# The last recurrent head of a hybrid decoder layer in steps of two block sizes

## The chip, the core and the metric

The kernel runs on one core of a Trainium2 chip. A core has five engines, each with its own in-order instruction queue: TensorE (PE; its weight loads are listed as PEld), VectorE (DVE), ScalarE (ACT), GpSimd (POOL) and SyncE (SP, which here issues nearly all transfers). They wait for one another through semaphores. Matmul results land in PSUM, in eight banks of 128 x 512 f32; everything else that is worked on lies in SBUF. The metric is the device time of one execution in microseconds.

## The reference

One decoder layer over 1024 tokens of width 1024, all in float32. After a normalisation, one projection feeds two mixers: dilated sliding-window attention of 8 heads, and a gated linear recurrence (HGRN2) of 4 heads of width 128. Their outputs are joined, projected and added to x; a squared-ReLU feed-forward layer follows. The recurrence, per head:

```python
def step(state, xs):                     # one chunk of C tokens
    qc, kc, vc, gc = xs                  # gc: log of the forget gate
    b = jnp.cumsum(gc, axis=2)
    o_inter = einsum('bhtk,bhkv->bhtv', qc * exp(b), state)
    decay = exp(where(causal, b_t - b_s, -inf))
    a = einsum('bhtk,bhsk,bhtsk->bhts', qc, kc, decay)
    o = o_inter + einsum('bhts,bhsv->bhtv', a, vc)
    new_state = exp(b_last) * state + einsum('bhsk,bhsv->bhkv', kc * exp(b_last - b), vc)
```

The kernel takes chunks of 128 tokens. What the change touches is how the 128 x 128 matrix `a` of a chunk, with its decay between every pair of tokens, is built.

## The kernel before

**Splits.** Large products run in three passes of a 32-bit format: both operands are split into a high and a low part (`split_into`, L85: ACT copies the high part, DVE subtracts, L87), and `three_pass` (L89 to L92) multiplies high x high, high x low, low x high. Weights stream in through `w_load` (L107) and `w_split`; `w_get` (L148) sees to it that a given weight block is split, each split being one long ACT and one long DVE instruction.

**Fillers.** The order of all engines is the order of the program text. Projections are Python generators in a `queue`; each yields after one unit (three matmuls of 128 x 512, booked at 650 ns, or 330 ns in `hgrn_ig`). `fill(ns)` (L195) lets the generators run until the booked costs reach `ns`; a debt or excess is carried on. A generator that yields `None` is blocked, and `fill` stops there. `drain` runs the queue empty.

**Recurrent heads.** For head h, `hgrn_core(h)` runs while the queue holds the projections of head h + 1 (`hgrn_ig`, evacuated by ACT at L421 and L422, and `hgrn_qf`, evacuated by DVE). For the last head, h = 3, the queue holds `attn_proj(0)` and `attn_proj(1)`, the projections of the first two pairs of attention heads, and all fills are scaled by 1.15. In `hgrn_core`: diagonal of `a` (L510, L511), then the climb over block sizes 1, 2, 4, ... 64, then the transposes of k (L615), the states (L623 to L629), the outputs `po` (L643, L645) with their squares (`ysq`, L647) and sums (`hss`, L648), and for the last head `open_attention`, which starts the scores of attention head 0 (`look`, L901, L902, read by DVE at L906; exponent on ACT, L959).

**The climb, two forms.** Between two neighbouring blocks of size c the entries of `a` are k times q, each scaled by running products of the gates.
- *By levels* (L584 to L609, last head): for each of seven sizes, 8 matmuls with 64 columns into one "s" bank (L593), then on DVE: scale half of k (L597), half of q (L599), multiply the totals (L603), and copy the wanted entries under a mask into `at` (L604). Then a fill: 3700, 2900, 2900, then 2200 four times.
- *Two sizes per step* (L519 to L583, heads 0 to 2): `quarter_sets` (L472) lays three operand sets side by side, per half four chunks wide, with two ACT copies and two DVE products (L483 to L490). A step is 8 matmuls with 192 columns into four banks (L529; tags "s", "t", "pv" in turn), the DVE products on q, totals, the next step's sets and k (L542 to L556), and twelve masked copies (L561), then two calls of `table_part` and two fills of 3500. Three steps cover sizes 1 to 32; size 64 is 8 matmuls of 64 x 64 (L572), an ACT copy (L574), three DVE products and a fill of 3400.

A matmul in f32 is issued as two passes, so 8 matmuls are 16 instructions in the profile.

**Attention projections.** `attn_proj(pr)` (L785) projects, for a pair, the queries in two halves (`aq`), the first half of the values (av), the keys in two halves (ak), then the second half of the values: 48 units a pair. Each half is 8 units in one bank with tag "mm" (two banks), which DVE reads out: queries at L806, values at L823, keys at L740. A buffer with tag "half" (two) receives it; for queries and keys ACT writes the high part into a second `half` buffer (`hiq`, `hik`, L733), POOL the low part (L734), and SP moves them into slabs (queries L811, L812; keys L750). Values are turned on PE into an "mm" bank (`pvt`, L773), four units into the next job, and read by ACT and DVE (L776, L777). `attn_proj(1)` blocks after its first half of the values until step 3 of attention.

**Slabs.** SBUF rows of 4 KB come from tags with a fixed number of buffers. Tag S has nine: in the last head it holds q, k, the totals and `at`, two queries per pair and four key slabs.

**After the last head** come 64 attention steps (L1349 on), each with a listed number of units (`UNITS`), one `fill(0.0, True)` per unit. Step 47 drains the queue and puts in the first part of the output projection; steps 44 to 48 also split weights for it on ACT and DVE (L140, L141).

Of the kernel before, what the change touches and what calls it, by code (L numbers as in the profile page):

```python
# [8 lines left out]
F32 = mybir.dt.float32  # L9
F32R = mybir.dt.float32r  # L10
U8 = mybir.dt.uint8
AF = mybir.ActivationFunctionType
ALU = mybir.AluOpType
# [4 lines left out]
P = 128  # L18
T = 1024
D = 1024  # L20
NK = D // P
NT = T // P
# [4 lines left out]
HH = 4  # L27
LEVELS = (1, 2, 4, 8, 16, 32, 64)
# [9 lines left out]
def hymba_layer(ctx, tc, x, w_in, w_out, w_ff1, w_ff2, g_pre, lb_logits, g_mix, g_post,  # L38
# [13 lines left out]
    def slab(tag, name, dtype=F32, shape=(P, T)):  # L52
        return sp.tile(list(shape), dtype, tag=tag, name=name,
                       bufs={"S": 9, "T": 9, "P": 3, "BT": 2, "V8": 2, "R": 1}[tag])

    def bank(tag, name):
        return ps.tile([P, 512], F32, tag=tag, name=name,
                       bufs={"mm": 2, "s": 2, "t": 2, "pv": 2}[tag])
# [136 lines left out]
    def fill(ns, least=False):  # L195
        debt[0] += ns
        if least:
            debt[0] = max(debt[0], 1.0)
        while debt[0] > 0 and queue:
            try:  # L200
                cost = next(queue[0])
            except StopIteration:
                queue.pop(0)
                continue
            if cost is None:
                break
            debt[0] -= cost
        debt[0] = min(debt[0], 0.0)
# [292 lines left out]
    def hgrn_core(h, scale, after=None):  # L501
        hd = heads[h]
        inat, gate, prod, qt, kt, tot = (hd[n] for n in ("inat", "gate", "prod", "qt", "kt", "tot"))
        ready = quarter_sets(hd, h, 0, tot) if h < HH - 1 else None
        fill((5900 if 0 < h < HH - 1 else 5200) * scale)
        at = slab("S", f"at{h}", F32, (P, NT, P))
        for hf in range(2):
# [7 lines left out]
            nc.sync.dma_start(out=gcols, in_=g_mix.rearrange("(k p) -> p k", p=P))  # L515
        if h == HH - 1:
            load_bias(0)
        if h < HH - 1:
            fill(1200 * scale)  # L519
            totals = slab("P", f"tot{h}")  # L520
            for step in range(3):
                c = 4 ** step
                nb = 32 // c
                sets, cv = ready
                banks4 = []
                for u in range(4):
                    pl = bank(("s", "t", "pv")[(2 * step + u // 2) % 3], f"pl{h}_{step}{u}").rearrange("p (n q) -> p n q", n=2)
                    for n in range(2 * u, 2 * u + 2):
                        TE.matmul(pl[:, n % 2, :192], kt[:, n * P:(n + 1) * P], sets[u // 2][:, n % 4],  # L529
                                  start=True, stop=True)  # L530
                    banks4.append(pl)
                w = T // (4 * c)
                at_ = (0, 768, 960)[step]
                tots = totals[:, at_:at_ + 3 * w].rearrange("p (i w) -> p i w", i=3)
                u23, u123, nx = (tots[:, i] for i in range(3))
                cw = cv.rearrange("p n b f -> p (n b) f")
                q4 = qt.rearrange("p (m f c) -> p m f c", f=4, c=c)
                k4 = kt.rearrange("p (m f c) -> p m f c", f=4, c=c)

                def spread(ap, k=c):  # L540
                    return ap.unsqueeze(2).to_broadcast([P, w, k])
                V.tensor_tensor(out=q4[:, :, 1], in0=q4[:, :, 1], in1=spread(cw[:, :, 0]), op=ALU.mult)  # L542
                for hf in range(2):
                    n4 = slice(hf * 4, hf * 4 + 4)
                    V.tensor_tensor(out=qt[:, hf * 512:hf * 512 + 512].rearrange("p (n b f c) -> p n b (f c)", n=4, f=4, c=c)
                                    [:, :, :, 2 * c:],
                                    in0=sets[hf][:, :, 128:].rearrange("p n (b w) -> p n b w", b=nb),
                                    in1=cv[:, n4, :, 0:1].to_broadcast([P, 4, nb, 2 * c]), op=ALU.mult)
                V.tensor_tensor(out=u23, in0=cw[:, :, 2], in1=cw[:, :, 3], op=ALU.mult)
                V.tensor_tensor(out=u123, in0=cw[:, :, 1], in1=u23, op=ALU.mult)  # L550
                V.tensor_tensor(out=nx, in0=cw[:, :, 0], in1=u123, op=ALU.mult)
                if step < 2:
                    ready = quarter_sets(hd, h, step + 1, nx)
                V.tensor_tensor(out=k4[:, :, 2], in0=k4[:, :, 2], in1=spread(cw[:, :, 3]), op=ALU.mult)
                V.tensor_tensor(out=k4[:, :, 1], in0=k4[:, :, 1], in1=spread(u23), op=ALU.mult)
                V.tensor_tensor(out=k4[:, :, 0], in0=k4[:, :, 0], in1=spread(u123), op=ALU.mult)  # L556
                for u, pl in enumerate(banks4):
                    for part_, mask, c2 in ((0, masks[:, 2 * step], c), (2, masks[:, 2 * step + 1], 2 * c),
                                            (1, near[:, step], 2 * c)):
                        av = at[:, 2 * u:2 * u + 2].rearrange("p n (b two c) -> p n b two c", two=2, c=c2)  # L560
                        V.copy_predicated(  # L561
                            av[:, :, :, 1, :],
                            mask.rearrange("p (b c) -> p b c", c=c2).unsqueeze(1).to_broadcast([P, 2, 64 // c2, c2]),
                            pl[:, :, part_ * 64:part_ * 64 + 64].rearrange("p n (b c) -> p n b c", c=c2))
                cur = nx
                table_part()
                fill(3500 * scale)
                table_part()
                fill(3500 * scale)
            pl = bank("s", f"pl{h}_6")  # L570
            for n in range(NT):
                TE.matmul(pl[:64, n * 64:(n + 1) * 64], kt[:, n * P:n * P + 64], qt[:, n * P + 64:(n + 1) * P],  # L572
                          start=True, stop=True)
            S.activation(at[:64, :, 64:], pl[:64].rearrange("p (n c) -> p n c", n=NT), AF.Copy)  # L574
            kv, qv = (x.rearrange("p (n two c) -> p n two c", two=2, c=64) for x in (kt, qt))
            cv = cur.rearrange("p (n two) -> p n two", two=2)
            V.tensor_tensor(out=qv[:, :, 1], in0=qv[:, :, 1], in1=cv[:, :, 0:1].to_broadcast([P, NT, 64]), op=ALU.mult)
            V.tensor_tensor(out=kv[:, :, 0], in0=kv[:, :, 0], in1=cv[:, :, 1:2].to_broadcast([P, NT, 64]), op=ALU.mult)
            nx = tp.tile([P, NT], F32, tag="tot8", name=f"tot{h}_8", bufs=1)
            V.tensor_tensor(out=nx, in0=cv[:, :, 0], in1=cv[:, :, 1], op=ALU.mult)  # L580
            cur = nx
            fill(3400 * scale)
        else:  # L583
            cur = tot  # L584
            fill(1200 * scale)
            for li, c in enumerate(LEVELS):
                nb = 64 // c
                qv = qt.rearrange("p (b two c) -> p b two c", two=2, c=c)
                kv = kt.rearrange("p (b two c) -> p b two c", two=2, c=c)
                av = at.rearrange("p n (b two c) -> p n b two c", two=2, c=c)  # L590
                pl = bank("s", f"pl{h}_{li}")
                for n in range(NT):
                    TE.matmul(pl[:, n * 64:(n + 1) * 64], kt[:, n * P:(n + 1) * P],  # L593
                              qv[:, n * nb:(n + 1) * nb, 1, :], start=True, stop=True)
                w = T // (2 * c)
                cv = cur[:, :2 * w].rearrange("p (b two) -> p b two", two=2)
                V.tensor_tensor(out=kv[:, :, 0, :], in0=kv[:, :, 0, :],  # L597
                                in1=cv[:, :, 1:2].to_broadcast([P, w, c]), op=ALU.mult)
                V.tensor_tensor(out=qv[:, :, 1, :], in0=qv[:, :, 1, :],  # L599
                                in1=cv[:, :, 0:1].to_broadcast([P, w, c]), op=ALU.mult)  # L600
                nx = slab("P", f"tot{h}_{w}") if w > 32 else \
                    tp.tile([P, w], F32, tag=f"tot{w}", name=f"tot{h}_{w}", bufs=1)
                V.tensor_tensor(out=nx[:, :w], in0=cv[:, :, 0], in1=cv[:, :, 1], op=ALU.mult)  # L603
                V.copy_predicated(  # L604
                    av[:, :, :, 1, :],
                    masks[:, li].rearrange("p (b c) -> p b c", c=c).unsqueeze(1).to_broadcast([P, NT, nb, c]),
                    pl.rearrange("p (n b c) -> p n b c", n=NT, c=c))
                cur = nx
                fill((3700 if li == 0 else 2900 if li < 3 else 2200) * scale)  # L609
        ktr = slab("T", f"ktr{h}", F32, (P, NT, P))  # L610
        for hf in range(2):
            pt = bank("t", f"pk{h}_{hf}")
# [1699 lines left out]
```

## Time and profile before

| | |
|---|---|
| median of 3 runs | 1205.58 us (1205.57 to 1205.9) |
| the profiled execution | 1205.52 us |
| its span, first to last instruction | 1203.5 us |
| PE, PEld, DVE, ACT, POOL busy | 1195.3, 1025.7, 849.7, 542.3, 294.7 us |
| L529 (192 columns), heads 0 to 2 | 144 instructions |
| L593 (64 columns), last head | 112 instructions, first and last start 251.6 and 283.8 us |
| last head, roughly | 242 to 305 us |
| attention steps, roughly | 304 to 520 us |

A line of a list of instructions begins with its start in us from the span's start and its length; then come the engine, the line of the kernel, the operation, output <- inputs with shapes, and how many were merged (x). Behind an instruction in brackets stand the idle time of its engine before it and what ended it. A line of the chain of waits has start, length and what ran. Matmuls are pipelined, so that their lengths overlap; what they take is read from starts or from the chain.

### The profile page before, as it was taken

Reading aid. Unit: us, or ns where it says so; the run is one execution under the profiler, and the core shown is the slowest. Engines: PE = TensorE matmul, PEld = TensorE weight load, DVE = VectorE, ACT = ScalarE, POOL = GpSimd, SP = SyncE. Lnnn points to the kernel's source line nnn. Section 1 sums busy time; section 2 is a strip of 40 time slices with the busy share of each in tenths; the row PEclk is TensorE's granted clock in tenths of the full one; section 3 lists DMA queues with packets and bytes.
Section 4 is the critical chain, followed back from the end, with each engine's and each line's share of the span. In section 5 each row is a group of like instructions: output and inputs, shape, how many; then the busy total and the mean of one; then the engine's idle time right before and its main releaser. Section 6 shows DMA issues by size and latency. Waiting matters only on the chain.

```text
span 1203.5 us, 17310 instructions
## 1 busy us (share of the span) xinstructions
PE 1195.3 (99%) x6342; PEld 1025.7 (85%) x6342; DVE 849.7 (71%) x1438; ACT 542.3 (45%) x1065; POOL 294.7 (24%) x280
## 2 busy tenths in 40 slices
PE   9999999999999999999999999999999999999997
PEld 9898989888888888888888888888888888888886
DVE  5696978775666767676599665766687553578796
ACT  7633333321565668855664222222234543434562
POOL 0121112010111110153421787575531000000022
PEclk9999999999999999999999999999999999999999
DMA  5222323135545556272524465553587534523337
GB/s 218 71 68 84 96 85 95 50 100 123 156 107 129 130 150 153 57 244 103 192 75 163 165 229 184 182 206 135 201 326 269 183 105 140 173 89 105 105 105 279
DMA packets 90547, 175.46 MB, mean 146 GB/s; under 512 B 14944, under 2 KB 42464, under 8 KB 90464
## 3 DMA queue, kind: packets, MB, share of 16 engines
q1 hardware_dynamic: 90320, 174.37, 45.6%
q8 instruction: 50, 0.82, 0.3%
q14 instruction: 33, 0.27, 0.1%
q10 hardware_dynamic: 144, 0.00, 0.0%
HBM read 116.91 MB, written 47.99 MB: 137 GB/s over the span
## 4 chain that ended last, share of the span: by engine, by line
PE 96%; ACT 2%; DVE 1%; issue 1%; DMA 0%; POOL 0%; DVEq 0%; POOLq 0%; ACTq 0%
PE f L2052 18%; PE f2s L2052 7%; PE pig L92 2%; PE pig L90 2%; PE pig L91 2%; PE pl L529 2%; PE pwo L90 2%; PE pwo L92 2%; PE pwo L91 2%; PE pm_ak L90 1%; PE pm_aq L90 1%; PE pm_f L90 1%; PE pm_aq L92 1%; PE pm_ak L92 1%; PE pm_ak L91 1%; PE pm_aq L91 1%
## 5 line engine op out<-in xcount | busy, mean ns | idle before, releaser
L87 DVE TENSOR_TENSOR al<-ar,ah 128x1024 fp32r<-128x1024 f32 x56 | 70.6, 1261 | 80.4 <-ACT ah L86 80.2
L2052 PE MATMUL f<-bh,ah 128*128 128x512 f32 x320 | 124.5, 389 | 0.0
L2052 PE MATMUL f<-bl,ah 128*128 128x512 f32 x320 | 124.5, 389 | 0.0
L2052 PE MATMUL f<-bh,al 128*128 128x512 f32 x320 | 124.5, 389 | 0.0
L86 ACT ACTIVATE ah<-ar 128x1024 fp32r<-128x1024 f32 x56 | 59.1, 1056 | 86.6 <-DMA ar<-actd 84.3
L2052 PEld LDWEIGHTS f<-bl,ah 128*128 128x128 f32 x320 | 60.1, 188 | 12.6
L2052 PEld LDWEIGHTS f<-bh,al 128*128 128x128 f32 x320 | 60.1, 188 | 12.5
L2052 PEld LDWEIGHTS f<-bh,ah 128*128 128x128 f32 x320 | 60.1, 188 | 12.3
L2126 POOL TENSOR_SCALAR lbl<-ssq 128x1 f32<-128x1 f32 x4 | 3.3, 820 | 245.7 <-ACT fd L2122 245.5
L1675 POOL TENSOR_TENSOR e<-x,e 128x512 f32<-128x512 f32 x14 | 21.6, 1541 | 131.0 <-DVE x L1626 123.8
L2052 PE MATMUL f2s<-bl,ah 128*128 128x512 f32 (+1 forms) x128 | 48.9, 382 | 0.0
L2052 PE MATMUL f2s<-bh,al 128*128 128x512 f32 (+1 forms) x128 | 48.9, 382 | 0.0
L2052 PE MATMUL f2s<-bh,ah 128*128 128x512 f32 (+1 forms) x128 | 48.9, 382 | 0.0
L718 POOL TENSOR_SCALAR tout<-traw 128x256 f32<-128x256 f32 x16 | 18.4, 1150 | 107.0 <-DMA traw<-in_bias_tab_dram 107.0
L87 DVE TENSOR_TENSOR bl<-br,bh 128x1024 fp32r<-128x1024 f32 x32 | 40.1, 1253 | 1.3 <-ACT bh L86 1.2
L2069 ACT ACTIVATE acc<-f 128x512 f32<-128x512 f32 x28 | 16.7, 598 | 49.5 <-PE f L2052 49.5
L86 ACT ACTIVATE bh<-br 128x1024 fp32r<-128x1024 f32 x32 | 33.6, 1050 | 4.3 <-PE f L2052 2.7
L87 DVE TENSOR_TENSOR wl<-raw,wh 128x1024 fp32r<-128x1024 f32 x21 | 25.9, 1233 | 10.2 <-ACT wh L86 10.2
L764 POOL TENSOR_TENSOR kl<-kf,kh 64x512 fp32r<-64x512 f32 x12 | 15.4, 1287 | 70.9 <-ACT kh L763 49.4
L90 PE MATMUL pwo<-woh,mt 128*128 128x512 f32 x80 | 32.2, 402 | 0.0
L92 PE MATMUL pwo<-woh,mt 128*128 128x512 f32 x80 | 31.3, 391 | 0.0
L91 PE MATMUL pwo<-wol,mt 128*128 128x512 f32 x80 | 31.2, 390 | 0.0
(1724 smaller groups left out, 3937.7 us busy)
## 6 DMA issues: line engine op xcount, KB each, us to landing
ar<-actd SPq DMA_DIRECT2D x56, 512.0 KB, 3.6
br<-in_w_ff_dram SPq DMA_DIRECT2D x16, 1024.0 KB, 5.8
raw<-in_w_in_dram SPq DMA_DIRECT2D x28, 512.0 KB, 4.1
w1r<-in_w_ff_dram SPq DMA_DIRECT2D x14, 1024.0 KB, 6.5
actd<-e SPq DMA_DIRECT2D x17, 768.0 KB, 4.3
actd<-e SPq DMA_DIRECT2D x11, 1024.0 KB, 4.1
xr<-in_x_dram SPq DMA_DIRECT2D x8, 512.0 KB, 8.0
raw<-in_w_out_dram SPq DMA_DIRECT2D x8, 512.0 KB, 3.7
```

The lines of the kernel that those rows point to most:

```text
L86: S.activation(hi, src, AF.Copy)
L87: eng.tensor_tensor(out=lo, in0=src, in1=f32(hi), op=ALU.subtract)
L90: TE.matmul(dst, lhs[0], rhs[0], start=start, stop=False)
L91: TE.matmul(dst, lhs[0], rhs[1], start=False, stop=False)
L92: TE.matmul(dst, lhs[1], rhs[0], start=False, stop=stop)
L529: TE.matmul(pl[:, n % 2, :192], kt[:, n * P:(n + 1) * P], sets[u // 2][:, n % 4], start=True, stop=True)
L718: G.tensor_scalar(by_class(dst[:, part_ * w:(part_ + 1) * w]), in_blocks(raw[:, FAR * DIL:]), 8.0, None, op0=ALU.mult)
L764: G.tensor_tensor(out=kl[a:b], in0=src, in1=f32(kh[a:b]), op=ALU.subtract)
L1675: eng[0].tensor_tensor(out=e1[:, 3], in0=a21, in1=e1[:, 2], op=ALU.add)
L2052: TE.matmul(pm, a[:, j, c], b[:, j, d], start=start and j == 0 and q == 0, stop=stop and j == 1 and q == 2, skip_group_check=True)
L2069: S.activation(acc_at(p, i), pm, AF.Copy)
L2126: G.tensor_scalar(base[:, t:t + 1], sums[j][:, t:t + 1], 1.0 / D, EPS, op0=ALU.mult, op1=ALU.add)
```

## The change

The last head takes the second form too. The test for it goes, with the whole branch by levels; the rest of the first branch moves one indent to the left, unchanged. The calls of `table_part` return at once in the last head, since the tables are finished in head 2. With the branch its seven fills go, 18300 in sum, and three times two of 3500 and one of 3400, 24400 in sum, take their place; the projections that no longer run in the attention steps run here.

```diff
-        ready = quarter_sets(hd, h, 0, tot) if h < HH - 1 else None
+        ready = quarter_sets(hd, h, 0, tot)
...
-        if h < HH - 1:
-            fill(1200 * scale)
-            totals = slab("P", f"tot{h}")
-            for step in range(3):
+        fill(1200 * scale)
+        totals = slab("P", f"tot{h}")
+        for step in range(3):
...
+            table_part()
+            fill(3500 * scale)
+            table_part()
+            fill(3500 * scale)
...
+        fill(3400 * scale)
-        else:
-            cur = tot
-            fill(1200 * scale)
-            for li, c in enumerate(LEVELS):
-                nb = 64 // c
-                qv = qt.rearrange("p (b two c) -> p b two c", two=2, c=c)
-                kv = kt.rearrange("p (b two c) -> p b two c", two=2, c=c)
-                av = at.rearrange("p n (b two c) -> p n b two c", two=2, c=c)
-                pl = bank("s", f"pl{h}_{li}")
-                for n in range(NT):
-                    TE.matmul(pl[:, n * 64:(n + 1) * 64], kt[:, n * P:(n + 1) * P],
-                              qv[:, n * nb:(n + 1) * nb, 1, :], start=True, stop=True)
-                w = T // (2 * c)
-                cv = cur[:, :2 * w].rearrange("p (b two) -> p b two", two=2)
-                V.tensor_tensor(out=kv[:, :, 0, :], in0=kv[:, :, 0, :],
-                                in1=cv[:, :, 1:2].to_broadcast([P, w, c]), op=ALU.mult)
-                V.tensor_tensor(out=qv[:, :, 1, :], in0=qv[:, :, 1, :],
-                                in1=cv[:, :, 0:1].to_broadcast([P, w, c]), op=ALU.mult)
-                nx = slab("P", f"tot{h}_{w}") if w > 32 else \
-                    tp.tile([P, w], F32, tag=f"tot{w}", name=f"tot{h}_{w}", bufs=1)
-                V.tensor_tensor(out=nx[:, :w], in0=cv[:, :, 0], in1=cv[:, :, 1], op=ALU.mult)
-                V.copy_predicated(
...
-                cur = nx
-                fill((3700 if li == 0 else 2900 if li < 3 else 2200) * scale)
```

More of the change, by code (lines that the diff above doesn't have):

```diff
@@ new lines, in hgrn_core @@
+        pl = bank("s", f"pl{h}_6")
+        for n in range(NT):
+            TE.matmul(pl[:64, n * 64:(n + 1) * 64], kt[:, n * P:n * P + 64], qt[:, n * P + 64:(n + 1) * P],
+                      start=True, stop=True)
+        S.activation(at[:64, :, 64:], pl[:64].rearrange("p (n c) -> p n c", n=NT), AF.Copy)
+        kv, qv = (x.rearrange("p (n two c) -> p n two c", two=2, c=64) for x in (kt, qt))
+        cv = cur.rearrange("p (n two) -> p n two", two=2)
+        V.tensor_tensor(out=qv[:, :, 1], in0=qv[:, :, 1], in1=cv[:, :, 0:1].to_broadcast([P, NT, 64]), op=ALU.mult)
@@ L610, in hgrn_core @@
+        V.tensor_tensor(out=kv[:, :, 0], in0=kv[:, :, 0], in1=cv[:, :, 1:2].to_broadcast([P, NT, 64]), op=ALU.mult)
+        nx = tp.tile([P, NT], F32, tag="tot8", name=f"tot{h}_8", bufs=1)
+        V.tensor_tensor(out=nx, in0=cv[:, :, 0], in1=cv[:, :, 1], op=ALU.mult)
+        cur = nx
+        fill(3400 * scale)
         ktr = slab("T", f"ktr{h}", F32, (P, NT, P))
```

104 lines of the change are left out of this document (42 added, 62 removed).

## The prediction

> **What bounds the kernel now.** I read the page's busy times and chain first, then the chain of waits in order of time, then the queues of the vector and scalar engines around the last recurrent head.
>
> ```profile
> span 1203.5 us, 17310 instructions
> PE 1195.3 (99%) x6342; PEld 1025.7 (85%) x6342; DVE 849.7 (71%) x1438; ACT 542.3 (45%) x1065; POOL 294.7 (24%) x280
> PEclk9999999999999999999999999999999999999999
> PE 96%; ACT 2%; DVE 1%; issue 1%; DMA 0%; POOL 0%; DVEq 0%; POOLq 0%; ACTq 0%
> 242.00:296.00 54.00, 54.00 (x311) 46.81 (x310) 37.37 (x61) 12.61 (x19) 6.62 (x5) 1.00 0.49 114
> ```
>
> TensorE (PE) ends the kernel and is never late: 96% of the chain is its own, and in the last head (242 to 296 us, last line: length, then PE busy) it is busy all the time. So the time changes by PE work saved, plus every wait that PE newly meets. VectorE (DVE) has 37.4 of 54 us there, so what it adds need not be free.
>
> **The work that goes.** The chain, start, length, what:
>
> ```profile
> 190.90 2.60 PE pl L529 x16
> 221.34 1.07 PE pl L572 x16
> 251.96 1.73 PE pl L593 x16
> 253.69 0.29 PE pm_aq L90
> 253.98 0.23 PE pm_aq L91
> 268.30 0.44 PE pvt L773 x4
> ```
> ```profile
> L593 PE MATMUL pl<-qt,kt 128*128 128x64 f32 x112 | 13.3, 271 | 0.0
> L529 PE MATMUL pl<-qs,kt 128*128 128x192 f32 x144 | 24.9, 326 | 0.0
> ```
>
> The 112 passes of L593 are seven groups of 16; each costs 1.73 and makes the next matmul 0.06 longer: 7 x 1.79 = 12.5. The new form is, per head, three groups of L529 and one of L572: 3 x 2.60 + 1.07 + 0.06 = 8.9. **PE saves 3.5 us.** The projections only move (one unit: three matmuls, 3 x 0.23 = 0.69), so they cost PE nothing themselves.
>
> Against this term speaks the Trainium skill, "TensorE: Matmul & The Clock Gate", section "Back-to-back issue gap": columns / 2.4 GHz + 2.5 ns, so 82.5 ns for 192 columns and 29.2 for 64. By that estimate the new groups cost 48 x 82.5 + 16 x 29.2 = 4.4 against 112 x 29.2 = 3.3, PE would lose 1.2, and the sum would be 1224.2. The rows have 163 and 108 ns a pass, so the trace does not agree, in size or in sign, and decides.
>
> **The DVE queue in the last head.** The second operands and the evacuation of projections share one in-order queue:
>
> ```profile
> 249.30 1.28 ACT L1312 ACT_TABLE_LOAD   x1
> 250.71 1.04 ACT L86 ACTIVATE wh<-raw 128x1024 fp32r<-128x1024 f32 x1
> 251.78 1.23 DVE L87 TENSOR_TENSOR wl<-raw,wh 128x1024 fp32r<-128x1024 f32 x1 [1.77 <-ACT wh L86]
> 254.72 1.53 DVE L597 TENSOR_TENSOR kt<-kt,tot 128x512 f32<-128x512 f32 x1
> 257.37 1.29 DVE L604 COPY_PREDICATED at<-masks,pl 128x512 f32<-128x512 uint8 x1
> 258.69 0.69 DVE L806 TENSOR_TENSOR qf<-pm_aq,rrow 128x512 f32<-128x512 f32 x1
> 253.70 0.63 ACT L733 ACTIVATE hiq<-qf 128x512 fp32r<-128x512 f32 x1 [0.25 <-DVE qf L806]
> ```
>
> L806 frees the "mm" bank of the second query half (aq0, hf 1), and runs only after the whole level has left DVE: a level takes 4 us here. Now the same part of head 2, whose steps are the new form:
>
> ```profile
> 187.80 0.42 ACT L483 ACTIVATE qs<-qt 128x256 f32<-128x256 f32 x1
> 189.10 1.05 ACT L86 ACTIVATE wh<-raw 128x1024 fp32r<-128x1024 f32 x1
> 192.55 0.62 DVE L542 TENSOR_TENSOR qt<-qt,tot 128x256 f32<-128x256 f32 x1
> 199.21 0.92 DVE L561 COPY_PREDICATED at<-masks,pl 128x128 f32<-128x128 uint8 x2
> 204.14 0.45 DVE L542 TENSOR_TENSOR qt<-qt,tot 128x256 f32<-128x256 f32 x1
> 209.01 0.61 DVE L561 COPY_PREDICATED at<-masks,pl 128x128 f32<-128x128 uint8 x2
> 212.44 0.42 DVE L542 TENSOR_TENSOR qt<-qt,tot 128x256 f32<-128x256 f32 x1
> 197.13 0.37 ACT L421 ACTIVATE inat<-pig,rstd 128x128 f32<-128x128 f32 x1 [2.47 <-PE pig L92]
> ```
>
> Step 0 takes DVE 11.6 us (6.66 to its first predicated copy, 4.93 for the twelve), step 1 8.3. In heads 0 and 1, 2 that hurts nobody: the work filled in there is emptied by ACT (last row). In the last head it is attention projections, emptied by DVE behind the step. Following the queue:
>
> - The first sets put four ACT copies (187.80 to 189.10: 1.3) ahead of the weight split at 250.71, on which DVE waits; step 0 starts at 254.7 + 1.3 = 256.0 and ends at 267.6. PE gets its first operand about 0.2 late: **0.2**.
> - PE: first group to 254.6, twelve units (two calls of 3500 x 1.15 at 650 each) to 262.9, second group. Its last quarter needs an "s" bank that two of four copy triples free at 256.0 + 6.66 + 2.47: **0.5**. PE is through at 266.0.
> - It then wants the first key unit (ak0): the bank is freed by L806, and the key weights' low part by L87; both stand behind step 0, and the split's ACT half behind hiq. 267.6 + 0.6 + 0.6 + 1.0 + 1.2 = 271.1, wanted at 266.4: **4.7**. In the kernel before, this wait was hidden by levels of 2 to 4 us.
> - vf follows (0.6), step 1 runs 271.7 to 280.0, then L777 frees the bank of the value transpose (0.6). PE reaches the second key half after seven units and pvt, 276.7: **3.9**. Step 2 is shorter and gives no third wait.
>
> That is 9.3. Bounds: 0 (DVE just in time) and 12 (a third wait like the second).
>
> **The end of the last head.** The fills now total 6100 x 1.15 = 7.0 us more: 69 units instead of 58 before attention, counted by their costs. So the eighth unit of aq1 falls in the fill after L615, not behind `po`, and its two query slabs (tag S, 9) are wanted while q, at, the four key slabs, two queries hold eight: the second waits until `po` is through. SP waits at that transfer; behind it, both `half` buffers, so the next L806 on DVE, hiq and `ysq` on ACT, `hss`, then the first score read.
>
> ```profile
> 300.54 0.31 PE L901 MATMUL ps_D<-kh,q 128*128 128x128 f32 x1
> 303.17 0.28 PE L901 MATMUL ps_N<-kh,q 128*128 128x256 f32 x1
> 300.82 0.60 ACT L647 ACTIVATE ysq<-po 128x512 f32<-128x512 f32 x1 [2.58 <-PE po L645]
> 301.45 0.69 DVE L648 TENSOR_REDUCE hss<-ysq 128x4 f32<-128x512 f32 x1 [2.49 <-ACT ysq L647]
> 302.05 0.28 DVE L906 CUSTOM_DVE_ANT_0 pd<-ps_D,bt 128x128 f32<-128x128 f32 x1
> 303.85 0.42 DVE L906 CUSTOM_DVE_ANT_0 pn<-ps_N,bt 128x256 f32<-128x256 f32 x1 [0.56 <-PE ps_N L902]
> 302.38 0.40 ACT L959 ACTIVATE pd<-pd,stat 128x128 f32<-128x128 f32 x1 [0.96 <-DVE stat L906]
> ```
> ```profile
> q<-hiq SPq DMA_DIRECT2D x16, 128.0 KB, 2.6
> ```
>
> From the end of `po`: 0.3 + 2.6 (landing) + 0.7 (L806) + 0.6 (hiq) + 0.6, 0.6 (ysq twice, the first reduction beside) + 0.7 (hss) + 0.3 (L906) = 6.5. PE wants the bank for ps_N at 303.17 - 300.54 = 2.6: **3.9**. The weight split of av1 now also stands before ps_N's read: 0.4 (exponent) + 1.0 + 1.2 + 0.8 (two L906), so the next ps_N finds its bank late by **1.7**. Steps 1 and 2 then have no filler (aq1 and its first value half are used up, the keys may start in step 3); the chain over L906 and the swap is bare: **1.0** as an estimate, between 0 and 1.5. Sum 6.6.
>
> ```profile
> 298.52 4.37 SPq L687 DMA_DIRECT2D vf<-vd  x6
> ```
>
> If the slab were free, SP would still come late to the query transfers: its far loads end at 302.9, 8 us after their transposes, and the fourth transfer would land about 1.6 us after L806 wants its buffer. With the bare chain of step 2 that leaves some **2.0**, the lower end; the upper is 9, if each link takes a third more.
>
> **The attention steps.** The eleven units that came forward are missing later, counted by the same costs: two in step 1, three in step 2, one in step 18, five in steps 45 to 47 (at 452 to 460 us).
>
> ```profile
> 447.00:460.00 13.00, 12.95 (x83) 11.13 (x83) 9.27 (x21) 12.09 (x35) 3.85 (x3) 1.00 0.51 118
> ```
>
> ACT (fifth number) is busy 12.09 of 13 us at 45 to 47, so five units less (3.4) leave PE waiting for exponents. It ran up to 1.3 us behind PE and one key split moves earlier: **1.5**, between 0 and 3.4. GpSimd's and SP's own load does not change; no later transfer is close to late, PE having no wait there.
>
> **Sum:** 1205.5 (the profiled execution, 2.0 more than its span and equal to the median of the runs) - 3.5 + 9.3 + 6.6 + 1.5 = **1219.4**.
>
> **Rivals.**
> - *The queue does not hold PE* (0.12): faster. One mechanism: L806 and L87 in step 0 done when PE wants the keys. It decides at 266.4; DVE would have to be 4.7 us sooner. Then the second wait and the buffers fall too: 1205.5 - 3.5 + 0 to 1.5, 1202.5. For it: DVE idle 16 us in the head. Against: the 11.6 us in one piece.
> - *In between* (0.08): only one wait of about 3.9 stays: 1205.9.
> - *The slab is no wait* (0.18), as when fewer units come forward than the costs say, which is the change not doing what it says: 2.0 instead of 6.6, so 1214.8.
> - *The clock falls* (0.14). In the trace PE has no gap like 3.9 to 4.7 and the clock reads 9 throughout, so this cannot be seen. If each of the three long waits were followed by as long a time at half speed, 12.5 x 0.5 = 6.2 more: 1225.6. The Trainium skill, "TensorE: Matmul & The Clock Gate", section "Why this matters for your kernels", has it that an idle gap over about 3 us brings the clock down to half.
> - *The forecast* (0.48): all waits, full clock, 1219.4.
>
> **Numbers.** What a measurement can tell from no change is about 0.2%, 2.4 us. Faster 0.12, same 0.08 (in between), slower 0.80. The first two are left out of the range; it runs from 1209, the slab rival with half the head's waits less, to 1227, the clock rival with the attention bound.
>
> **What would show it.** Right: PE idle some 5 us before pm_ak with DVE wl as releaser, some 4 before its second half on DVE v (L777), some 4 before ps_N on DVE stat; SP waiting on PE at L811; pl groups of 2.60; slices 9 or 10 of PE below 9. Wrong: PE busy through the last head, or L806 directly behind its matmuls. It would be wrong as a whole if DVE's step is shorter without the tables on GpSimd.

## The result and the profile after

The changed kernel takes **1226.37 us** (median, 1224.45 to 1226.57, 4 runs) against 1205.74 (1205.57 to 1206.46, 4 runs) for the kernel before beside it: ratio 1.0166, 95% interval 1.0149 to 1.0184. It is slower by 20.6; forecast were 13.9. From here on line numbers are those of each kernel itself. In the changed kernel the steps are one line lower and what follows the head is 28 lower: L806 is L778, L777 is L749, L823 is L795, L901 is L873, L906 is L878, L811 is L783.

The page of the changed kernel: span, busy time, the 40 slices of PE and of its granted clock, and the chain's shares by engine.

```profile
span 1224.3 us, 17277 instructions
PE 1201.4 (98%) x6294; PEld 1027.3 (84%) x6294; DVE 855.7 (70%) x1488; ACT 545.8 (45%) x1078; POOL 294.8 (24%) x280
PE   9999999988899999999999999999999999999998
PEclk9999999989999999999999999999999999999999
PE 91%; DVE 4%; ACT 2%; issue 1%; DMA 1%; POOL 0%; DVEq 0%; POOLq 0%; SPq 0%; ACTq 0%
```

Slices 9 to 11 (245 to 337 us) have lost PE's time, the chain is 5 points less PE, and slice 9 has a clock under 0.90, which no slice had. In the kernel before, the row of PE was:

```profile
PE   9999999999999999999999999999999999999997
```

From the view of the waits of PE (tile and line that waited, releaser: us in all, times, longest):

```profile
PE pm_ak L90 <- ACT wh L86: 3.6, 1, 3.6
PE pm_ak L90 <- DVE v L749: 3.5, 1, 3.5
PE ps_N L873 <- DVE stat L878: 3.0, 1, 3.0
PE pt_N L950 <- ACT pn L931: 1.2, 2, 0.9
PE ps_F L873 <- DVE stat L878: 1.2, 1, 1.2
PE ps_D L873 <- DVE stat L878: 0.7, 1, 0.7
PE px L912 <- DVE swap L905: 0.4, 1, 0.4
```

The three long waits stand where they were forecast, before the first key unit, before the second key half (on L749) and before the first ps_N. The releaser of the first is not the one forecast: it is ScalarE's half of the weight split (wh, 3.6); VectorE's half (wl), which was named, adds 0.3. What they wait for is seen in VectorE's timeline (start, length, what, idle time before it and its releaser):

```profile
268.00 0.71 DVE L778 TENSOR_TENSOR qf<-pm_aq,rrow 128x512 f32<-128x512 f32 x1
270.36 1.45 DVE L87 TENSOR_TENSOR wl<-raw,wh 128x1024 fp32r<-128x1024 f32 x1 [1.64 <-ACT wh L86]
273.91 0.69 DVE L795 TENSOR_TENSOR vf<-pm_av,rrow 128x512 f32<-128x512 f32 x1 [2.10 <-DMA q<-hiq]
...
282.32 0.68 DVE L749 TENSOR_TENSOR v<-pvt,v 128x512 fp32r<-128x512 f32 x1
```

L778 runs at 268.0, behind all twelve copies of step 0 (forecast: 267.6). The third line was not foreseen: the value half needs a half buffer, both are still read by query transfers, and step 1 starts 2.1 us later for it. In TensorE's timeline the same three places are:

```profile
270.38 0.80 PE L90 MATMUL pm_ak<-hTh,wh 128*128 128x512 f32 x1 [3.60 <-ACT wh L86]
...
283.06 0.80 PE L90 MATMUL pm_ak<-hTh,wh 128*128 128x512 f32 x1 [3.53 <-DVE v L749]
...
287.37 2.76 PE L528 MATMUL pl<-qs,kt 128*128 128x192 f32 x16
...
318.00 0.31 PE L873 MATMUL ps_D<-kh,q 128*128 128x128 f32 x1
...
323.77 0.58 PE L873 MATMUL ps_N<-kh,q 128*128 128x256 f32 x1 [2.97 <-DVE stat L878]
```

Busy times by stretch (from:to, length, PE, PEld, DVE, ACT, POOL; then PE's granted clock) show what followed each wait:

```profile
270.40:276.50 6.10, 5.84 (x16) 4.19 (x17) 3.89 (x9) 1.12 (x4) 0.32 (x1) 0.54 0.70 176
283.00:287.00 4.00, 3.94 (x11) 3.16 (x12) 3.14 (x8) 0.63 (x1) 1.34 (x1) 0.60 0.73 164
322.00:326.00 4.00, 2.23 (x8) 2.11 (x9) 2.61 (x7) 2.74 (x8) 2.90 (x3) 0.72 0.59 125
326.00:340.00 14.00, 12.38 (x62) 10.00 (x61) 9.75 (x42) 5.58 (x16) 0.00 (x0) 0.84 0.37 104
```

The clock did fall. The twelve passes from 283.06 to 287.37 took 4.3 us, where twelve passes at 0.23 are 2.8.

**Two places at which all kernels can be compared** are the first score product (ps_D, opens attention) and the first far product (pov_far). Their starts, less 0.69 us for each projection unit that the trace has ahead of them beyond the kernel before, split the loss into three: up to ps_D is the head, from there to pov_far its end, and the rest lies in attention. For pov_far the rows of the tile, first in the kernel before and then in the changed one, each in a window of its trace (durations, then first and last start of the matmuls):

```profile
L1033 PE MATMUL pov_far<-ptFh,vf x12: 221/274/277, 320.5 to 348.1; 128*128 128x128 f32 x12
```
```profile
L1005 PE MATMUL pov_far<-ptFh,vf x8: 220/274/280, 343.5 to 347.4; 128*128 128x128 f32 x8
```

Head: 318.0 - 300.5 - 11 x 0.69 = 9.9. To pov_far: 343.5 - 320.5 - 6 x 0.69 = 18.9, so the end has 9.0. The spans differ by 20.8, so attention (all that lies behind) has 1.9. (The forecast's terms for the three: 9.3 - 3.5 = 5.8, 6.6 and 1.5.) All kernels so; time and starts in us, units and starts from the profiled run (that of evac_late is the fastest of its four runs, 1223.0, that of at_in_p the slowest, 1228.3):

| kernel | time | units ahead of ps_D / pov_far | ps_D | head | pov_far | head and end |
|---|---|---|---|---|---|---|
| before | 1205.6 | 55 / 74 | 300.5 | 0 | 320.5 | 0 |
| after | 1226.4 | 66 / 80 | 318.0 | 9.9 | 343.5 | 18.9 |
| form_only | 1219.3 | 55 / 74 | 314.9 | 14.3 | 334.8 | 14.3 |
| units_only | 1219.1 | 66 / 80 | 309.6 | 1.5 | 336.3 | 11.6 |
| evict_mid | 1221.7 | 66 / 80 | 313.6 | 5.5 | 339.1 | 14.4 |
| stay_busy | 1224.7 | 66 / 80 | 316.4 | 8.2 | 341.9 | 17.3 |
| at_in_p | 1226.0 | 66 / 80 | 317.8 | 9.7 | 342.4 | 17.7 |
| vf_own | 1223.6 | 66 / 80 | 314.4 | 6.2 | 339.9 | 15.3 |
| spread69 | 1220.3 | 66 / 80 | 308.9 | 0.8 | 334.2 | 9.6 |
| evac_late | 1225.2 | 64 / 80 | 316.9 | 10.1 | 340.3 | 15.6 |
| units_late | 1212.8 | 62 / 80 | 306.9 | 1.6 | 330.1 | 5.4 |
| spread58 | 1209.5 | 55 / 74 | 303.7 | 3.1 | 323.6 | 3.1 |
| tuned58 | 1206.4 | 55 / 74 | 301.3 | 0.8 | 321.3 | 0.8 |
| hybrid58 | 1204.6 | 55 / 74 | 299.7 | -0.9 | 319.6 | -0.9 |

### The profile page after: what moved, and what is told of

It is laid out like the page before. It is cut to its first block, busy times and chain, and to the rows that moved or that the text cites. A ratio compares the mean times of both kernels' runs of the same rounds, so it can differ in the third digit from the quotient of the medians.

```text
span 1224.3 us, 17277 instructions
## 1 busy us (share of the span) xinstructions
PE 1201.4 (98%) x6294; PEld 1027.3 (84%) x6294; DVE 855.7 (70%) x1488; ACT 545.8 (45%) x1078; POOL 294.8 (24%) x280
## 4 chain that ended last, share of the span: by engine, by line
PE 91%; DVE 4%; ACT 2%; issue 1%; DMA 1%; POOL 0%; DVEq 0%; POOLq 0%; SPq 0%; ACTq 0%
PE f L2024 18%; PE f2s L2024 7%; PE pig L92 2%; PE pig L90 2%; PE pig L91 2%; PE pl L528 2%; PE pwo L92 2%; PE pwo L90 2%; PE pwo L91 2%; PE pm_ak L90 1%; PE pm_ak L92 1%; PE pm_ak L91 1%; PE pm_av L90 1%; PE pm_f L90 1%; PE pm_aq L90 1%
## 5 line engine op out<-in xcount | busy, mean ns | idle before, releaser
L90 PE MATMUL pm_ak<-hTh,wh 128*128 128x512 f32 x64 | 29.9, 467 | 7.1 <-ACT wh L86 3.6
L560 DVE COPY_PREDICATED at<-masks,pl 128x128 f32<-128x128 uint8 x96 | 33.5, 349 | 1.6
L528 PE MATMUL pl<-qs,kt 128*128 128x192 f32 x192 | 33.6, 327 | 0.6 <-DVE at L560 0.3
L528 PEld LDWEIGHTS pl<-qs,kt 128*128 128x128 f32 x192 | 31.0, 190 | 1.8 <-issue 1.3
```

Of the source, the lines that this page charges most:

```text
L90: TE.matmul(dst, lhs[0], rhs[0], start=start, stop=False)
L560: V.copy_predicated(av[:, :, :, 1, :], mask.rearrange("p (b c) -> p b c", c=c2).unsqueeze(1).to_broadcast([P, 2, 64 // c2, c2]), pl[:, :, ...
```

## The experiments

The theory to test, A: VectorE's in-order queue holds the projections' banks and weights in the head; the slab holds the end of the head; the units that came forward are missing in attention; and the waits lower the clock.

### One half of the change each

**form_only** has the new steps with the old sum of fills, **units_only** the old levels with the new sum.

```diff
-            fill(3500 * scale)
+            fill((2600 if h == HH - 1 else 3500) * scale)
...
-        fill(3400 * scale)
+        fill((2700 if h == HH - 1 else 3400) * scale)
```


> The new steps in the last head, with the fills cut back to the sum of the kernel before (six of 2600 and one of 2700), so that 58 units run before attention as in the kernel before. Theory A (VectorE's queue holds the projections, the eleven units hold the end of the head and the attention steps, each long wait lowers the clock): the waits in the last head stay, in part at other places because PE now reaches the next step's operands sooner: -3.5 for PE, +6 to 9 of waits, +2 to 4 of clock, so 1210 to 1216; no wait of 3 us before ps_N, and no more than before in steps 45 to 47. Theory B (the whole loss comes from the eleven units that run early): 1202.

1219.3 us, ratio 1.0115 (1.010 to 1.013).

```diff
-                fill((3700 if li == 0 else 2900 if li < 3 else 2200) * scale)
+                fill((4600 if li == 0 else 3800 if li < 3 else 3050) * scale)
```


> The kernel before, with its seven levels in the last head, and only the fills raised by 6100 in sum, so that 69 units run before attention as in the changed kernel. Theory A: the end of the head and the attention steps lose what they lose in the changed kernel, 5 us of waits at the end of the head, 2.4 in attention, 3 of clock, and nothing in the steps: 1213 to 1217. Theory B (all of it is the units): 20.6 + 3.5 more than before, about 1229. Theory C (all of it is the new steps): 1206.

1219.05 us, ratio 1.0113 (1.0098 to 1.0128). Theory B (units alone) and theory C (steps alone) fall: each half costs 13 to 14. Both lie above what theory A gave them, and together they lose 27.3, not 20.6. The table says why. The form alone loses everything in the head, 14.3, and nothing behind it; the units alone lose 1.5 in the head and 10.1 at its end. Put together, the head loses less (9.9): with fewer units between its groups TensorE comes sooner to what VectorE has not finished. The waits of form_only:

```profile
PE pvt L745 <- DVE vf L795: 4.3, 1, 4.3
PE pl L528 <- DVE kt L555: 2.3, 1, 2.3
PE pm_ak L90 <- ACT wh L86: 1.6, 1, 1.6
```

The value half now stands behind step 1, and the next group's operand comes late too. The projections are a cover for the steps as well as their victim.

### The order on VectorE

**evict_mid** issues the first fill of a step after half of its copies.

```diff
                         pl[:, :, part_ * 64:part_ * 64 + 64]...)
+                if h == HH - 1 and u % 2:
+                    table_part()
+                    fill(3500 * scale)
```


> The changed kernel, with the same order on TensorE, but in the last head the first of the two fills of a step is issued after half of the predicated copies instead of after all, so that VectorE empties the projections before the other half. Theory A: L778 and what follows it come 2.5 us sooner, the bank of the value transpose 1.8 us sooner: the waits before pm_ak fall from 3.6 and 3.5 to 1 to 2 each, and the low clock behind them goes for the most part: 1217 to 1220. Rival (those waits are set by the weight load or by the transfers that free the half buffers, not by the copies): 1225 to 1227.

1221.7 us (1220.0 to 1224.4), ratio 1.0137: 4.7 less than the changed kernel, where 6 to 9 were expected. The first wait fell to 2.4 in two parts, at full clock. L749 ran 4.4 us sooner:

```profile
277.93 0.68 DVE L753 TENSOR_TENSOR v<-pvt,v 128x512 fp32r<-128x512 f32 x1
```

But TensorE, no longer slowed, was there as much sooner, and still waited 3.2.

**vf_own** gives the first value half a buffer of its own.

```diff
-            full = half(f"vf{pr}{hf}")
+            full = slab("P", f"vf{pr}{hf}")[:, :512] if pr == hf == 0 else half(f"vf{pr}{hf}")
```


> The changed kernel, but the first value half of the first pair (vf, L795) is written to a slab of the tag P instead of a half buffer, so that it no longer waits for the query transfers that still read both half buffers. Theory A (VectorE stands 2.1 us at L795 for a transfer ahead of step 1, and step 1 holds the second half of the keys): step 1 starts 2 us sooner, the wait before the second half of the keys falls from 3.5 to about 1.4, and the low clock behind it (1.5 us) goes: 1222 to 1224. Rival (those 2.1 us are slack, since the copies of step 1 or the value transpose set that wait): 1225.5 to 1227.

1223.6 us, ratio 1.0148 (1.0133 to 1.0164), as expected. PE's timeline of that kernel:

```profile
280.90 0.50 PE L90 MATMUL pm_ak<-hTh,wh 128*128 128x512 f32 x1 [1.60 <-DVE v L749]
```
```profile
283.00:287.00 4.00, 4.00 (x24) 3.76 (x23) 1.45 (x5) 0.00 (x0) 0.59 (x1) 1.00 0.97 209
```

The wait ends 2.2 sooner than at 283.06, the clock behind it is full, and ps_D comes 3.6 sooner. So the buffer's 2.1 us were on the path.

**spread69** has four pieces of fill per step, with the same order on TensorE.

```diff
+            piece = (1750, 1750, 1750)[step] * scale
+            if tail:
+                fill(piece)
...
                 ready = quarter_sets(hd, h, step + 1, nx)
+            if tail:
+                fill(piece)
...
+            if tail:
+                fill(piece)
             for u, pl in enumerate(banks4):
...
+                if tail and u == 1:
+                    fill(piece)
```


> The changed kernel with all its 69 units and the same order on TensorE, but the fills of a step of the last head are issued in four pieces: after the group's products, after the next sets, before the copies, and after half of the copies. So VectorE empties the projections inside the step. Theory A (it is VectorE's order, not its load, that holds the keys): up to the first ps_D the kernel comes 6 to 10 us sooner than the changed kernel, the waits before pm_ak go under 1.5 each; the end of the head and the attention steps lose 9 and 2 as before: 1216 to 1220. Rival (VectorE has too much work in the head, and a wait that goes comes back before the next group): 1222 to 1226.

1220.25 us (1217.2 to 1222.7), ratio 1.0119 (1.0104 to 1.0134), a quarter of a us above what theory A gave and well below the rival. The first score product, at 318.00 in the changed kernel with as many units ahead of it, starts 9.1 sooner:

```profile
308.91 0.31 PE L884 MATMUL ps_D<-kh,q 128*128 128x128 f32 x1
```

The head loses 0.8 instead of 9.9, so order it is, not load. The end kept its 8.8, and the profiled run met a low clock in attention too, which the changed kernel had not there:

```profile
466.00:480.00 14.00, 12.52 (x65) 10.83 (x64) 10.97 (x30) 10.34 (x29) 0.00 (x0) 0.76 0.25 76
```

### What the low clock costs

**stay_busy** puts products of zeros into the three long waits; their results are not used.

```diff
+    def stay_busy(n, w=256):
+        pw = bank("t", f"pw{done[1]}_{keys_done[0]}")
+        for _ in range(n):
+            TE.matmul(pw[:, :w], zero.to_broadcast([P, P]), zero.to_broadcast([P, w]), start=True, stop=True)
...
+            if pr == 0:
+                stay_busy(6)
             for n, cost in enumerate(proj_t(wk, f"ak{pr}", hf, box)):
...
+            stay_busy(6)
             look(0, "N", 0)
```


> The changed kernel, with six products of zeros of 256 columns put before each half of the first key projection and before the first ps_N, at the three places where TensorE waits for 3.0 to 3.6 us. They add some 2.6 us of work at each place, inside the wait, and change nothing else. Clock theory (the low granted clock after those waits comes from the idle time and costs 7 us): the granted clock stays at 1.00 in these stretches, and the time falls to 1219 to 1222 although work is added. Rival (the waits alone are the loss, the clock reading only goes with the idle time): 1226 to 1229.

1224.7 us (1224.6 to 1226.3), ratio 1.0162: between the two. The clock behaved as the clock theory has it; these rows are those of the stretches shown above:

```profile
270.40:276.50 6.10, 5.15 (x23) 3.64 (x24) 3.89 (x9) 1.34 (x5) 0.19 (x1) 1.00 0.71 174
283.00:287.00 4.00, 4.00 (x20) 3.50 (x21) 3.00 (x7) 0.64 (x1) 1.36 (x1) 1.00 0.78 172
322.00:326.00 4.00, 2.34 (x13) 1.82 (x14) 2.83 (x12) 2.62 (x7) 1.80 (x2) 1.00 0.79 185
326.00:340.00 14.00, 12.45 (x69) 10.69 (x68) 9.26 (x37) 6.49 (x21) 0.00 (x0) 0.88 0.28 79
```

The price did not. The second key half starts where it did. The two score products into ps_N come 1.6 sooner, but no nearer to each other:

```profile
282.90 0.50 PE L90 MATMUL pm_ak<-hTh,wh 128*128 128x512 f32 x1 [2.34 <-DVE v L750]
...
322.13 0.38 PE L881 MATMUL ps_N<-kh,q 128*128 128x256 f32 x1 [0.36 <-DVE stat L886]
...
325.56 0.39 PE L881 MATMUL ps_N<-kh,q 128*128 128x256 f32 x1 [1.52 <-DVE stat L886]
```

In the changed kernel these are 283.06, 323.77 and 327.19, and nearly all of the difference of 1.6 in the last two arose between 283 and 287, behind the second wait: the group at 287.37 there starts at 285.76 here. The slow stretch behind the first wait ends in a wait for VectorE, and the one behind the third too, where the second ps_N now waits 1.5: there a faster TensorE only waits longer. Of the low clock directly behind the three long waits 1.6 us were on the path. From 326 us on the clock is low in both kernels, so this run says nothing of its price there.

### The end of the head

**at_in_p** frees the ninth slab.

```diff
-        at = slab("S", f"at{h}", F32, (P, NT, P))
+        at = slab("P" if h == HH - 1 else "S", f"at{h}", F32, (P, NT, P))
```


> The changed kernel with all its 69 units, but in the last head the slab of at comes from the tag P, which has one free there, so that nine slabs of the tag S hold both query slabs of aq1 and nobody waits for po. Theory A (the second query slab waits for po, and SP's transfer, the half buffer, the exponent's and the square's chain hold ps_N): the 3.0 us before ps_N go to under 1, the low clock behind them goes, and the later waits on the score reads stay in part: 1219 to 1222. Rival (the end of the head loses because aq1's units bring transfers and reads of their own, or because the fillers are missing behind it): 1225 to 1227.

1226.0 us (1222.1 to 1228.3), ratio 1.0165 (1.0147 to 1.0182): the rival. Below are SP's third query transfer of the pair's first half and VectorE's next L778, first in the changed kernel, then here:

```profile
318.05 0.46 SPq L783 DMA_DIRECT2D q<-hiq  x1
320.36 0.69 DVE L778 TENSOR_TENSOR qf<-pm_aq,rrow 128x512 f32<-128x512 f32 x1 [8.28 <-DMA q<-hiq]
```
```profile
313.33 0.55 SPq L783 DMA_DIRECT2D q<-hiq  x1
319.37 0.69 DVE L778 TENSOR_TENSOR qf<-pm_aq,rrow 128x512 f32<-128x512 f32 x1 [7.45 <-DMA q<-hiq]
```

The transfer goes out 4.7 us sooner, and its buffer is free only 1.0 sooner: SP now issues it right behind six far loads and a 512 KB weight load, and it lands later. That these hold it is read from the order of the issues; it was not tried apart. The DMA view from 305 to 326 us has 2.3 us from issue to landing (median) in the changed kernel and here

```profile
q<-hiq SPq DMA_DIRECT2D x4, 128.0 KB, 4.2
```

The slab is a wait, but not the one that counts: with it free the end of the head still loses 8.0 (17.7 - 9.7) of its 9.0.

**evac_late** moves 1300 of fill from ahead of po to behind the first score reads.

```diff
-        fill(2600 * scale)
+        fill((1200 if h == HH - 1 else 2600) * scale)
         sq = slab("P", f"ysq{h}", F32, (P, NT, P))
...
-        fill(1500 * scale)
+        fill((2900 if h == HH - 1 else 1500) * scale)
```


> The changed kernel with all its 69 units before attention, but 1300 of the fill ahead of po is moved behind the head's first two score reads, so that VectorE's read of the second query half of aq1 (the second L778 of that pair) and its exponent-side copy stand behind the squares, hss and the first reads of the scores instead of ahead of them. The transfers, the slab and the units stay. Theory A' (in place of the slab alone: whatever makes that L778 late, the slab or the transfers behind the far loads and the weight load, it is its place in VectorE's queue ahead of hss that holds ps_N): the 3.0 us before ps_N go, half or more of the 9 us lost between the first ps_D and the first far product go with them: 1219 to 1223. Rival (the reads of the scores lack the fillers behind them, or wait for that L778 at the next bank): the wait returns one or two reads later, 1224.5 to 1227.

1225.2 us (1223.0 to 1225.5), ratio 1.0159. This edit missed its aim: L778 came to stand between the two squares, and the wait was split into 1.1 and 1.5. The time lies in the rival's range, but with the order not as it was meant it says nothing between the theories. By chance it shows something else: behind the split wait the clock stayed at 1.00, and the end of the head lost 5.5 (15.6 - 10.1, 4.1 of it waits) instead of 9.0.

**units_late** does it fully, and in the kernel with the old levels, where the head hides nothing.

```diff
-        fill(2600 * scale)
+        fill((1200 if h == HH - 1 else 2600) * scale)
...
-                fill(1500 * scale)
+                fill((500 if h == HH - 1 else 1500) * scale)
...
-        fill(1500 * scale)
+        fill((3900 if h == HH - 1 else 1500) * scale)
```


> The run with the old levels and 69 units, in which only the end of the head and the attention steps lose (1219.05; 4.1 us before the first ps_N), with the fills around po moved: 1200, 500 and 3900 in place of 2600, 1500 and 1500, so that the second query half of aq1 ends behind the head's first two score reads. Its read by VectorE then stands behind the squares, both hss and those two reads, which the run with the changed kernel's order did not reach (there it still stood between the two squares, and the wait was split into 1.1 and 1.5). Theory A' (the place in VectorE's queue holds ps_N): no wait before the first ps_N, 1 to 3 us left before the next reads: 1213 to 1216.5. Rival (the reads of the scores come late anyway, since the transfers behind the far loads hold VectorE at the next place): 1217.5 to 1220.

1212.8 us, ratio 1.0064 (1.005 to 1.0078), 6.3 less than units_only and a little better than theory A' gave. units_only had

```profile
PE ps_N L901 <- DVE stat L906: 4.1, 1, 4.1
```

as its longest wait; here no wait for ps_N is left. VectorE:

```profile
308.45 0.28 DVE L906 CUSTOM_DVE_ANT_0 pd<-ps_D,bt 128x128 f32<-128x128 f32 x1
...
309.29 0.69 DVE L806 TENSOR_TENSOR qf<-pm_aq,rrow 128x512 f32<-128x512 f32 x1 [0.21 <-DMA q<-hiq]
```

The first score read stands ahead of the query half, which finds its buffer free. It is the place in VectorE's queue that held the end of the head. (po also comes four units sooner here, so that the transfers are sooner out. But the buffer comes free 2.4 us behind the start of ps_D, at 309.29 against 306.9, where in units_only it was 3.3, at 312.9 against 309.6: that is 0.9 of a wait of 4.1.) Of the end's 10.1 us 3.8 stay, with waits of 1.2 before ps_F and 0.4 before px; how they divide between absent fillers and a clock of 0.84 to 0.87 was not tried.

### A version without the waits

**spread58** is spread69 with the old sum of fills.

```diff
-            piece = (1750, 1750, 1750)[step] * scale
+            piece = (1750, 1400, 900)[step] * scale
...
-        fill(3400 * scale)
+        fill((2100 if h == HH - 1 else 3400) * scale)
```


> As the run with the fills in four pieces, with 58 units before attention as in the kernel before (pieces of 1750, 1400 and 900 in the three steps, and 2100 behind them). Theory A: neither the end of the head nor the attention steps lose anything, and the head loses 0 to 4 against 3.5 that TensorE saves: 1202 to 1207. Rival (VectorE's load in the head): the form costs what it cost with 58 units in two pieces, in part at other places, 1212 to 1219.

1209.45 us, ratio 1.0033 (1.002 to 1.0045): between the two. The end of the head and attention lose nothing; waits of 1.9, 1.6 and 1.1 are left in the head.

**tuned58** moves two of its pieces, and 1300 of fill from behind the transposes of k to ahead of them.

```diff
-            if tail:
-                fill(piece)
             V.tensor_tensor(out=k4[:, :, 2], ...)
...
-                if tail and u == 1:
+                if tail and u in (1, 3):
                     fill(piece)
...
-        fill((2100 if h == HH - 1 else 3400) * scale)
+        fill((3400 if h == HH - 1 else 3400) * scale)
...
-        fill(3000 * scale)
+        fill((1700 if h == HH - 1 else 3000) * scale)
```


> As the run with the fills in four pieces and 58 units; the second piece comes after the multiplications of the keys, so that the next group's operand is not behind a read of a projection, the fourth after all copies, and 1300 of filler stands ahead of the transposes of the keys instead of behind them. Theory A (order holds PE: 1.9 before the second group and 1.6 before the transposes go): 1205 to 1207.5. Rival (VectorE's load: in that run it worked 33.7 us without a break from 256.1 to 289.8, so a wait that goes at one place returns at the next): 1208.5 to 1210.5.

1206.43 us, ratio 1.0006 (0.9997 to 1.0015): order again. One long wait, of 1.6 before the second key half, is left, and four short ones of 0.2 to 0.4.

**hybrid58** is tuned58 with sizes 1 and 2 by levels, and with the pieces of fill fitted to that.

```diff
+        if tail:
+            for li, c in enumerate(LEVELS[:2]):
...
+                if li == 1:
+                    ready = quarter_sets(hd, h, 1, nx[:, :w])
...
-        for step in range(3):
+        for step in range(1 if tail else 0, 3):
```


> In the last head the sizes 1 and 2 by the old levels, and the new steps only for 4, 8 and 16, 32, with the fills in pieces as in the run before this, 58 units before attention. VectorE is spared the long first step. TensorE saves 7 x 1.79 - (2 x 1.79 + 2 x 2.70 + 1.13) = 2.4. Theory A (the long first step is what made VectorE late): waits of 0 to 2, so 1203 to 1206. Rival (any step of the new form holds the keys' reads): 2 to 5 of waits, 1206 to 1209.

1204.58 us, ratio 0.9993 (0.9984 to 1.0002), not told apart from the kernel before, and the only version that isn't slower in its median. It is what its theory gave (1203 to 1206), but as the fills moved as well, it does not show alone that the long first step was what remained. Its waits in the head are

```profile
PE pk L623 <- DVE kt L613: 0.7, 1, 0.7
PE pl L556 <- DVE qs L490: 0.3, 1, 0.3
```

## Why the prediction was right, and where it was not

**Direction and mechanism** held: PE saves a little and meets three waits of 3 to 4 us and several short ones. The three stand at the places that were named; the second and third have the releaser that was named, the first has ScalarE's half of the weight split in place of VectorE's. Of the 20.8 us between the spans 13.9 were forecast, so the sum was 6.9 short. The steps in turn:

- *PE saves 3.5.* The groups took what was forecast (2.5 from 287.37 to the next matmul). The whole saving is seen nowhere alone: hybrid58 should have gained 2.4 less its waits of 1.0, and is 0.9 ahead at ps_D. The other price that the prediction had for these groups, and its sum of 1224.2, is nearer to the time by luck only: by it a group would take 1.3, and it took 2.5.
- *The last head, 9.3: measured 13.4* (9.9 + 3.5, if the saving is granted in full). The first group came 0.2 late, as forecast; the second waited 0.3 for its operand, which was not in the sum, and 0.3 for its bank, for 0.5. The first key wait was 3.6 + 0.3 for 4.7. The second should have ended at 280.6 and ended at 283.1; that its length was nearly right (3.5 for 3.9) is luck, since TensorE came to it 2.8 later as well, with eight units ahead of it, not seven, and a low clock. The step that failed is "vf follows (0.6)": it took no account of the half buffers, which cost 2.1 there. The slow clock after that wait added 1.5. Without these two the step would have been right within half a us; in vf_own both are gone, and the head loses 3.7 less.
- *The end of the head, 6.6: measured 9.0.* From ps_D to the first ps_N it loses 3.1, to the second 1.8, to pov_far 4.1; the terms were 3.9, 1.7 and 1.0. The wait before the first ps_N was 3.0 for 3.9, with L778, hiq, the squares and hss in the order that was written down. The holder was named wrongly: "the second waits until po is through" is true (SP waits 5.5 us there) and nearly idle: with the slab free (at_in_p) the same buffer came free only 1.0 earlier, with the far loads and the weight load issued ahead of its transfer. The rival that made the slab decide between 6.6 and 2.0 falls with it: with the slab free it was 8.0. What cures the wait is the order (units_late). The 1.7 before the second ps_N is there, but as slow passes; with the clock held up (stay_busy) the same time is a wait of 1.5 for VectorE. The term that was mis-sized is the 1.0 for the bare steps: 1.2 and 0.4 of waits stand there, and the other 2.5, by difference, go with a clock of 0.84.
- *Attention, 1.5: measured 1.9*, within its bounds. In PE's timeline:

```profile
476.02 0.44 PE L950 MATMUL pt_N<-ident,pn 128*128 128x128 f32 x2 [0.33 <-ACT pn L931]
...
477.36 0.44 PE L950 MATMUL pt_N<-ident,pn 128*128 128x128 f32 x2 [0.90 <-ACT pn L931]
...
479.59 0.39 PE L873 MATMUL ps_D<-kh,q 128*128 128x256 f32 x1 [0.70 <-DVE stat L878]
```

 These are 1.9 in all; the kernels with 58 units lose nothing behind the head.
- *Full clock.* This failed: the granted clock was 0.54 to 0.84 behind the waits. The time came out at the price of the clock rival (1225.6), but not by its sum. It priced each slow stretch in full; of those directly behind the three long waits 1.6 was on the path, and the rest of the gap to the forecast is the half buffer (2.1) and, at the end of the head, the short waits and the low clock from 326 us on. A right number with a part of its reason wrong; and as the range ended at 1227 with that rival's sum, that 1226.4 lies just inside it is luck in part.

## What to carry to other kernels

When work moves to an engine's in-order queue, ask which reads stand behind it there: here the same instructions, with TensorE's order untouched and only VectorE's reads (with the splits and transfers that go with them) moved up, took 9.1 us out of the head. Units that fill one place are missing in another, and a cover that shrinks lets TensorE run into waits it had not had. A slow stretch of an engine costs only if the next wait isn't for someone else: price it from its end, not from its length.

## What was not expected of the hardware

Around and behind waits of 3.0 to 3.6 us the granted clock was 0.54 to 0.72 in stretches of 4 to 6 us, and a pass of 512 columns took 0.43 us instead of 0.23. It also fell without such a wait: in stay_busy it was 0.88 from 326 to 340, where the waits are 1.2 and 0.4, one of 1.5 just ahead; in evac_late the same three waits left it at 1.00. Some kernels with waits vary more from run to run as well: spread69 took 1217.2 to 1222.7 us with a mean clock of 0.996 to 0.989, the kernel before 1205.3 to 1207.2. The Trainium skill, "TensorE: Matmul & The Clock Gate", section "What's actually happening", lets a free-running window of 3413 ns decide, so that the phase in which a wait falls matters; these two kernels agree with that better than with the bound of about 3 us between bursts that the prediction took from that page, though no run here shows the window itself. The prediction had no place for chance in the clock.

Products of zeros keep the clock up: with six of them in each wait it read 1.00 where it had been 0.54, 0.60 and 0.72.
